# Low parts made by TensorE and ScalarE, a larger priority offset, and conv_out in two lots of token tiles, in a two-layer trunk

## The chip, the cores and the metric

One Trainium2 chip; the kernel is one launch on one of its cores. The metric is the device time of one execution in microseconds, the median of several runs. The engines are TensorE (PE; PEld is its weight load), VectorE (DVE), ScalarE (ACT), GpSimd (POOL) and SyncE (SP), which issues most of the DMAs. Each takes its own instructions in order and waits on semaphores for the others.

## The reference

1024 tokens of width 1024 pass two layers. Layer 0 mixes tokens with an S5 state-space model and a GLU, layer 1 with a gated short convolution. A SwiGLU FFN (hidden width 2816) and a per-layer input gate (PLE) follow each mixer, every sub-layer is normalised ahead, and all is float32.

```python
def shortconv_mixer(u, w_in, w_conv, w_out):
    b_gate, c_gate, v = jnp.split(u @ w_in, 3, axis=-1)
    cv = c_gate * v
    conv = lax.conv_general_dilated(cv, w_conv[:, None, :], ...)
    return (b_gate * conv) @ w_out

def swiglu_ffn(u, w_in, w_out):
    gate, up = jnp.split(u @ w_in, 2, axis=-1)
    return (jax.nn.silu(gate) * up) @ w_out
# per layer: x += mixer(rmsnorm(x)); x += ffn(rmsnorm(x)); x += ple(rmsnorm(x), p); last a final rmsnorm
```

## The kernel before, in words

**Precision.** Each float32 operand is split into a high part, a cast to fp32r on ScalarE, and a low part, the operand less its high part on VectorE (`split`, L86 to L88). A product is three matmuls: high by high, high by low, low by high (`mm3`, L121 to L124).

**Tiles.** The residual stream `h` is eight tiles of 128 tokens, t = 0 to 7, taken in the order 0, 4, 1, 5, 2, 6, 3, 7; tiles q and q + 4 are pair q. The phases are S5 and GLU, FFN 0 (in, out), PLE 0, conv_in, conv_out, FFN 1, PLE 1. `conv_in` and `ffn_in` use a block product of the Strassen kind (`block_product`, L289 to L318): seven products of half-size blocks in place of eight, with seven moving operands of 512 tokens, `moving(0)` to `moving(6)`. 0, 3 and 5 are plain blocks of the normalised tokens (p11, p21, p22); 1, 2, 4 and 6 are sums of blocks (T2, T1, T3, T4).

**The transitions.** `norm_pair` (L207 to L233) makes the moving operands of one pair. It normalises both tiles into `xn` (L173, VectorE; the statistic is L144 and L146 on VectorE and a power on GpSimd, L148), transposes them on TensorE into four PSUM tiles (L181), and from these makes b12 (a copy on ScalarE, L219), T1 (L221), T2 (L223), T3 (L228), T4 (L232) and the seven splits (`put`, by L87 and L88). p11 and p21 come from the pair's first tile, p12 and p22 from its second. PSUM has three buffers for p11, p12 and p22 (pool `tr`) and five for products and p21 (pool `mm`).

It runs at three places, where one phase hands its tokens to a block product: GLU to FFN 0, PLE 0 to conv_in, conv_out to FFN 1. Pairs 0, 1 and 2 follow tiles 1, 2 and 3, pair 3 follows tile 7, the last. Each moving operand spans all four pairs.

**Weights.** `weights_set` (L258 to L284) loads two raw tiles and makes the seven stationary operands `ws` from them: casts on ScalarE, subtractions at L88, and sums at L275, L276, L278 and L283 on VectorE. The raw tiles, the hidden tiles `ch` and the normalised tiles `xn` share a ring of four slots (`raw_tile`, L92).

**Order of the work.** The tile framework orders each engine's instructions by a simulated timeline and by priority. `first()` (L128) raises the priority of what it encloses by an offset: the statistics, `xn`, and each phase's last add into `h` (L503 in the GLU, L435 in PLE, L360 in conv_out). The order is fixed when the kernel is built.

**conv_out** (L541) goes through `out_phase` (L326): two groups of four weight units, and for each group all eight token tiles. Units 0 to 3 lie in `ulow`, one in each pair's part; units 4 to 7 are made between the first group's tiles. A tile's second group adds to `h`, takes the squares and calls `post`.

**split_pe** (L251 to L255), so far used in S5 alone, makes a low part without VectorE: the cast of the PSUM tile (L253), a matmul that adds minus the high part to the same PSUM tile (`identn` is minus the identity, L254), and a cast of what is left (L255).

Of the kernel before, what the change touches and what calls it, by code (L numbers as in the profile page):

```python
# [23 lines left out]
def trunk(  # L24
# [54 lines left out]
    hdram = dram.tile([T, P, D], F32, name="hd")  # L79
    hid = [dram.tile([T, P, 4, 2, P], F32, name=f"hid{i}") for i in range((NHT + 3) // 4)]  # L80

    def psum(pool=None):
        pool = pool or mm
        return pool.tile([P, 512], F32, name="ps" + pool.name, tag="ps")

    def split(hi, lo, src):  # L86
        A.copy(hi, src)  # L87
        V.tensor_tensor(lo, src, hi.bitcast(F32), ALU.subtract)  # L88
# [27 lines left out]
    def unit_of(slot, raw):  # L116
        hi, lo = slot
        split(hi, lo, raw)
        return hi, lo

    def mm3(ps, ahi, alo, bhi, blo, start, stop, more=False):  # L121
        PE.matmul(ps, ahi, bhi, start=start, stop=False, skip_group_check=more)  # L122
        PE.matmul(ps, ahi, blo, start=False, stop=False, skip_group_check=more)  # L123
        PE.matmul(ps, alo, bhi, start=False, stop=stop, skip_group_check=more)  # L124
# [2 lines left out]
    squares = {}  # L127

    def first():
        return tc.high_priority(offset=100)  # L130

    def square(t, cs):

        if "ms" not in squares:
            squares["ms"] = tiny.tile([P, T, 4], F32, name="ms", tag="ms")
        got = squares.setdefault(t, [])
        junk = t2_tile("junk", BF16, D)
        ms = squares["ms"][:, t, len(got):len(got) + 1]
# [25 lines left out]
    def act(kt, t):  # L164
        return act_view(kt, 0, t), act_view(kt, 1, t)
# [10 lines left out]
    def transposed(xn, hf, pool=None):  # L176

        pt = psum(pool or tr)
        for c in range(KH):
            kt = hf * KH + c  # L180
            PE.transpose(pt[:, c * P:(c + 1) * P], xn[:, kt * P:(kt + 1) * P], ident)  # L181
# [25 lines left out]
    def norm_pair(q, gb):  # L207
        t0, t1 = q, q + HT
        halves = 2 if q == HT - 1 else 1
        x0, x1 = normed(t0, gb, halves), normed(t1, gb, halves)  # L210

        def put(c, src):
            split(moving_part(c, 0, q), moving_part(c, 1, q), by_kt(src))

        p11, p12, p22 = transposed(x0, 0), transposed(x1, 0), transposed(x1, 1)
        p21 = transposed(x0, 1, mm)
        put(0, p11)
        b12 = t2_tile("b12")
        A.copy(b12, p12)  # L219
        T1 = t2_tile("T1")  # L220
        V.tensor_tensor(T1, b12, p11, ALU.subtract)  # L221
        T2 = t2_tile("T2")
        V.tensor_tensor(T2, p22, T1, ALU.subtract)  # L223
# [22 lines left out]
    def transposes(pt, parts):  # L246
        for c, a in enumerate(parts):
            PE.matmul(pt[:, c * P:(c + 1) * P], a, ident, start=c == 0, stop=True, is_transpose=True,
                      skip_group_check=c > 0)

    def split_pe(hi, lo, pt, view=lambda a: a):  # L251

        A.copy(hi, view(pt))  # L253
        PE.matmul(pt, identn, hi, start=False, stop=True, skip_group_check=True)  # L254
        A.copy(lo, view(pt))  # L255
# [114 lines left out]
    def room_low(q, s):  # L370
        return lambda: slot_low(q, s)
# [4 lines left out]
    def room_new(i):  # L376
        return lambda: slot_new(i)
# [37 lines left out]

    def ple(l, units, post):
        more, makers = ple_units(l, 1, [room_new(i) for i in range(4)])
        for nb in range(2):
            cs = slice(nb * 512, (nb + 1) * 512)
            if nb == 1:  # L420
                units = more
            for t in ORDER:
                upt = t2_tile("upt")
                nc.sync.dma_start(out=upt, in_=updram[l][:, t, cs])
                last = l == 1 and t == ORDER[-1] and nb == 1
                for c0, c1 in ((0, 256), (256, 512)) if last else ((0, 512),):
                    ps = psum()[:, 0:c1 - c0]
                    for kt in range(KT):
                        bhi, blo = units[kt // 2]
                        mm3(ps, *act(kt, t), bhi[:, kt % 2, c0:c1], blo[:, kt % 2, c0:c1], kt == 0, kt == KT - 1)  # L430
                    with first():
                        A.activation(ps, ps, AF.Sigmoid)
                        V.tensor_tensor(upt[:, c0:c1], ps, upt[:, c0:c1], ALU.mult)
                        hc = slice(nb * 512 + c0, nb * 512 + c1)
                        V.tensor_tensor(h[t][:, hc], upt[:, c0:c1], h[t][:, hc], ALU.add)  # L435
                        square(t, hc)
                if nb == 0 and makers:
                    makers.pop(0)()
                if nb == 1:
                    post(t)  # L440
# [40 lines left out]
    def glu(post):  # L481
        wg = s5_w_glu[0].rearrange("(kt p) (two n) -> p kt two n", p=P, two=2)
        rooms = [[room_high(i) for i in range(4)], [room_new(i) for i in range(4)],
                 [room_high(i) for i in (4, 5, 0, 1)], [room_new(i) for i in range(4)]]
        for nb in range(4):
            cs = slice(nb * 256, (nb + 1) * 256)
            units = []
            for u in range(KT // 2):
                raw = raw_tile()
                rv = raw.rearrange("p (kt two n) -> p kt two n", kt=2, two=2)  # L490
                for k in range(2):
                    nc.sync.dma_start(out=rv[:, k], in_=wg[:, 2 * u + k, :, cs])
                units.append([a.rearrange("p (kt n) -> p kt n", kt=2) for a in unit_of(rooms[nb][u](), raw)])
            for t in ORDER:
                ps = psum()
                for kt in range(KT):
                    bhi, blo = units[kt // 2]
                    mm3(ps, *act(kt, t), bhi[:, kt % 2, :], blo[:, kt % 2, :], kt == 0, kt == KT - 1)
                sg = t2_tile("sgg")[:, 0:256]
                with first():  # L500
                    A.activation(sg, ps[:, 256:512], AF.Sigmoid)
                    V.tensor_tensor(sg, ps[:, 0:256], sg, ALU.mult)
                    V.tensor_tensor(h[t][:, cs], sg, h[t][:, cs], ALU.add)  # L503
                    square(t, cs)
                if nb == 3:
                    post(t)
# [591 lines left out]
```

## Time and profile before

| | us |
|---|---|
| median of 3 runs | 2354.29 (2352.39 to 2357.11) |
| the profiled execution | 2359.43 |
| its span on the core | 2357.5 |
| TensorE busy | 2247.0 (95%) |
| VectorE busy | 1331.9 (56%) |
| ScalarE busy | 765.5 (32%) |
| GpSimd busy | 163.1 (7%) |

A row of the timeline gives start, duration, engine, line, operation, out<-in, form and count, and in brackets the idle time before it with what ended it. A row of the windows gives the window, its length, then for PE, PEld, DVE, ACT and POOL the busy time and in brackets the instructions, the granted TensorE clock, the DMA share and GB/s. A row of the waits gives who waited and for whom, the time in all, how often, and the longest. A row for one line of code gives the smallest, median and largest duration in ns. Matmuls overlap: one takes 0.39 us from its start, but the next starts 0.23 later.

### The profile page before, as it was taken

The page shows a single profiled execution, that of the slowest core. Times are in us where ns is not written, and L with a number is a line of the kernel's source. Part 1 is how long each engine was busy: PE and PEld are TensorE (multiplying, and loading weights), DVE is VectorE, ACT ScalarE, POOL GpSimd, SP SyncE. Part 2 cuts the span into 40 slices and gives each one's busy share as a digit, 9 for nine tenths or more (in the row PEclk, how much of TensorE's full clock was granted, in tenths as well). Part 3 has the DMA queues.
Part 4 walks back from the last instruction along what each step waited for, and adds up shares of the span by engine and source line. Part 5 has one row for each costly group of instructions (what it writes and reads, how often), then busy time and mean ns, then how long its engine had stood idle before and what let it go on. Part 6 is the DMA issues. An engine that isn't in the chain of part 4 may idle for free.

```text
span 2357.5 us, 27090 instructions
## 1 busy us (share of the span) xinstructions
PE 2247.0 (95%) x10253; PEld 1835.7 (78%) x10253; DVE 1331.9 (56%) x2246; ACT 765.5 (32%) x1449; POOL 163.1 (7%) x268
## 2 busy tenths in 40 slices
PE   6888999899999999999979999989999999999998
PEld 4776887788888878878858888768888888788787
DVE  7785326866666642125488776487666666121454
ACT  6554223433333320013343332153333333000232
POOL 2110001000000000000000000010000001000000
PEclk8999999999999999999989999999999999999999
DMA  7555202333333364333232225434333335543333
GB/s 246 141 135 148 69 1 89 105 112 112 111 114 110 107 241 149 118 127 114 70 129 81 90 92 179 159 125 125 108 108 107 111 113 172 212 139 107 108 109 110
DMA packets 212978, 288.87 MB, mean 123 GB/s; under 512 B 21360, under 2 KB 152432, under 8 KB 212848
## 3 DMA queue, kind: packets, MB, share of 16 engines
q1 hardware_dynamic: 191520, 212.63, 29.0%
q0 software_dynamic: 20928, 74.47, 10.2%
q8 instruction: 80, 1.31, 0.2%
q14 instruction: 50, 0.41, 0.1%
q10 hardware_dynamic: 400, 0.04, 0.0%
HBM read 190.93 MB, written 79.69 MB: 115 GB/s over the span
## 4 chain that ended last, share of the span: by engine, by line
PE 85%; DMA 6%; DVE 5%; ACT 1%; SPq 1%; issue 1%; POOL 0%; DVEq 0%; POOLq 0%; ACTq 0%
PE psmm L122 27%; PE psmm L124 27%; PE psmm L123 27%; DMA ch<-hid 2%; PE pstr L181 1%; DMA raw<-in_ffn_w_out_dram 1%; DMA tw<-tmp 1%; DVE W L575 1%; DVE gv L925 1%; DMA h<-hd 1%; DVE tmp L575 1%; DVE ulow L88 1%; DVE uhigh L88 1%; PE pstr L874 0%; DVE raw L575 0%
## 5 line engine op out<-in xcount | busy, mean ns | idle before, releaser
L122 PE MATMUL psmm<-ulow,ws 128*128 128x512 f32 x896 | 351.1, 393 | 1.6 <-ACT s L301 1.6
L123 PE MATMUL psmm<-ulow,ws 128*128 128x512 f32 x896 | 350.6, 391 | 0.0
L124 PE MATMUL psmm<-ulow,ws 128*128 128x512 f32 x896 | 350.4, 391 | 0.0
L124 PE MATMUL psmm<-uhigh,ws 128*128 128x512 f32 x672 | 265.3, 395 | 0.0
L122 PE MATMUL psmm<-uhigh,ws 128*128 128x512 f32 x672 | 265.1, 394 | 0.0
L123 PE MATMUL psmm<-uhigh,ws 128*128 128x512 f32 x672 | 264.9, 394 | 0.0
L360 DVE TENSOR_TENSOR h<-psmm,h 128x512 f32<-128x512 f32 x128 | 88.0, 690 | 276.6 <-PE psmm L124 276.6
L88 DVE TENSOR_TENSOR ws<-raw,ws 128x512 fp32r<-128x512 f32 x224 | 153.6, 688 | 117.8 <-ACT ws L87 117.4
L87 ACT CAST ws<-raw 128x512 fp32r<-128x512 f32 x224 | 137.5, 619 | 213.0 <-PE psmm L124 211.2
L122 PEld LDWEIGHTS psmm<-ulow,ws 128*128 128x128 f32 x896 | 169.4, 189 | 39.5 <-ACT s L301 2.9
L123 PEld LDWEIGHTS psmm<-ulow,ws 128*128 128x128 f32 x896 | 169.4, 189 | 36.2
L124 PEld LDWEIGHTS psmm<-ulow,ws 128*128 128x128 f32 x896 | 169.2, 189 | 36.2
L87 ACT CAST ws<-st 128x512 fp32r<-128x512 f32 x168 | 104.0, 620 | 204.4 <-PE psmm L124 189.5
L123 PEld LDWEIGHTS psmm<-uhigh,ws 128*128 128x128 f32 x672 | 126.1, 188 | 30.3
L124 PEld LDWEIGHTS psmm<-uhigh,ws 128*128 128x128 f32 x672 | 126.1, 188 | 30.3
L122 PEld LDWEIGHTS psmm<-uhigh,ws 128*128 128x128 f32 x672 | 126.1, 188 | 29.1
L323 POOL DMA_DIRECT2D hid<-hs x104 | 78.2, 755 | 903.4 <-DVE hs L88 895.4
L122 PE MATMUL psmm<-ulow,ch 128*128 128x512 f32 x320 | 128.4, 401 | 10.8 <-DMA ch<-hid 10.8
L139 ACT ACTIVATE junk<-h 128x512 bf16<-128x512 f32 (+1 forms) x113 | 64.0, 567 | 204.0 <-DVE h L360 104.0
L87 ACT CAST uhigh<-raw 128x1024 fp32r<-128x1024 f32 x36 | 37.2, 1049 | 278.9 <-PE psmm L124 136.7
L123 PE MATMUL psmm<-ulow,ch 128*128 128x512 f32 x320 | 127.6, 399 | 0.0
L124 PE MATMUL psmm<-ulow,ch 128*128 128x512 f32 x320 | 127.5, 398 | 0.0
(240 smaller groups left out, 4238.5 us busy)
## 6 DMA issues: line engine op xcount, KB each, us to landing
hid<-hs POOLq DMA_DIRECT2D x104, 512.0 KB, 4.3
ch<-hid SPq DMA_DIRECT2D x96, 512.0 KB, 3.7
raw<-in_ffn_w_in_dram SPq DMA_DIRECT2D x88, 512.0 KB, 4.4
raw<-in_ffn_w_out_dram SPq DMA_DIRECT2D x44, 512.0 KB, 3.6
hd<-h POOLq DMA_DIRECT2D x24, 512.0 KB, 3.0
h<-hd SPq DMA_DIRECT2D x24, 512.0 KB, 8.7
raw<-in_conv_w_in_dram SPq DMA_DIRECT2D x24, 512.0 KB, 4.0
up<-ev SPq DMA_DIRECT2D x32, 256.0 KB, 3.2
```

The costliest lines, as they stand in the source:

```text
L87: A.copy(hi, src)
L88: V.tensor_tensor(lo, src, hi.bitcast(F32), ALU.subtract)
L122: PE.matmul(ps, ahi, bhi, start=start, stop=False, skip_group_check=more)
L123: PE.matmul(ps, ahi, blo, start=False, stop=False, skip_group_check=more)
L124: PE.matmul(ps, alo, bhi, start=False, stop=stop, skip_group_check=more)
L139: A.activation(junk[:, cs], h[t][:, cs], AF.Square, scale=1.0 / math.sqrt(D), accum_out=ms)
L181: PE.transpose(pt[:, c * P:(c + 1) * P], xn[:, kt * P:(kt + 1) * P], ident)
L323: nc.gpsimd.dma_start(out=hid[ht // 4][half * HT:(half + 1) * HT, :, ht % 4].rearrange("t p l j -> p t l j"), in_=hs.bitcast(F32))
L360: V.tensor_tensor(h[t][:, cs], ps[nb], h[t][:, cs], ALU.add)
L575: V.tensor_tensor(o, a, b, op)
L925: V.tensor_tensor_scan(gv[:, g, 1:P], dec, sv[:, g, 1:P], 0.0, ALU.mult, ALU.add)
```

## The change

Four edits. (1) `put` may make a low part by `split_pe`, and does so for the plain blocks, operands 0, 3 and 5; the transposes are written as matmuls (`transposes`); T1 stands ahead of operand 0 in the code, T4 ahead of operand 3. (2) The offset of `first()` goes from 100 to 400. (3) The loops of the GLU and PLE are flattened. (4) conv_out has its own loop: token tiles 0, 4, 1, 5 take both groups of weights, then 2, 6, 3, 7; units 0 to 3 lie in the parts of pairs 2 and 3 of `ulow` alone, and units 4 to 7 are made during the first lot's first group. In the new file the lines of before shift: T1 is L230, T2 L233, T4 L237, T3 L240, the transposes L258, split_pe L263 to L265, `mm3` L123 to L125, the sums of `weights_set` L285, L286, L288 and L293, the low parts L89, `xn` L174, the last adds L516 (GLU), L442 (PLE) and L576 (conv_out).

```diff
 def first():
-    return tc.high_priority(offset=100)
+    return tc.high_priority(offset=400)
...
-        def put(c, src):
-            split(moving_part(c, 0, q), moving_part(c, 1, q), by_kt(src))
-
-        p11, p12, p22 = transposed(x0, 0), transposed(x1, 0), transposed(x1, 1)
-        p21 = transposed(x0, 1, mm)
-        put(0, p11)
+        def put(c, src, on_pe=False):
+            hi, lo = moving_part(c, 0, q), moving_part(c, 1, q)
+            if on_pe:
+                split_pe(hi, lo, src, by_kt)
+            else:
+                split(hi, lo, by_kt(src))
+
+        def part(xn, hf, pool=tr):
+            pt = psum(pool)
+            transposes(pt, [xn[:, (hf * KH + c) * P:(hf * KH + c + 1) * P] for c in range(KH)])
+            return pt
+
+        p11, p12, p22 = part(x0, 0), part(x1, 0), part(x1, 1)
+        p21 = part(x0, 1, mm)
         b12 = t2_tile("b12")
         A.copy(b12, p12)
         T1 = t2_tile("T1")
         V.tensor_tensor(T1, b12, p11, ALU.subtract)
+        put(0, p11, True)
         T2 = t2_tile("T2")
         V.tensor_tensor(T2, p22, T1, ALU.subtract)
         put(1, T2)
         put(2, T1)
-        put(3, p21)
+        T4 = t2_tile("T4")
+        V.tensor_tensor(T4, p21, T2, ALU.subtract)
+        put(3, p21, True)
         T3 = t2_tile("T3")
         V.tensor_tensor(T3, p22, b12, ALU.subtract)
         put(4, T3)
-        put(5, p22)
-        T4 = t2_tile("T4")
-        V.tensor_tensor(T4, p21, T2, ALU.subtract)
+        put(5, p22, True)
         put(6, T4)
...
     def conv_out(post):
-        rooms = [(room_low(q, 0), False) for q in range(HT)] + [(room_new(i), True) for i in range(4)]
-        hts = [(ct, *room) for ct, room in enumerate(rooms)]
-        out_phase(conv_w_out[0].rearrange("(ht p) n -> ht p n", p=P), [hts[0:4], hts[4:8]], post)
+        rooms = [room_low(2 + i // 2, i % 2) for i in range(4)] + [room_new(i) for i in range(4)]
+        units = {}
+        def make(ct):
+            units[ct] = unit_of(rooms[ct](), load_raw(conv_w_out[0, ct * P:(ct + 1) * P], "p n -> p n"))
+        for ct in range(KH):
+            make(ct)
+        for i, t in [(i, t) for ts in (ORDER[:4], ORDER[4:]) for i in range(2) for t in ts]:
+            ch = raw_tile(shape=(P, 4, 2, P), dt=F32R, name="ch")
+            nc.sync.dma_start(out=ch.bitcast(F32), in_=hid[i][t])
+            if i == 0:
+                nc.sync.dma_start(out=h[t], in_=hdram[t])
+            for nb in range(2):
+                ...
+            if len(units) < KT:
+                make(len(units))
+            if i == 1:
+                post(t)
```

The order in which the engines get their instructions changes with it. On TensorE, at the end of the GLU, before: the last matmuls of the GLU (`w`, the GLU's weights), the transposes of pairs 2 and 3, and the first product of FFN 0 (`ulow,ws`).

```order
L123 MATMUL psmm<-w_3164,ulow 128x512
L124 MATMUL psmm<-w_3164,ulow 128x512
L181 MATMUL pstr<-ident,xn 128x128 x8
L181 MATMUL psmm<-ident,xn 128x128 x4
L181 MATMUL pstr<-ident,xn 128x128 x12
L122 MATMUL psmm<-ulow,ws 128x512
L123 MATMUL psmm<-ulow,ws 128x512
L124 MATMUL psmm<-ulow,ws 128x512
```

Afterwards the same place, with the identity matmuls (`identn`):

```order
L124 MATMUL psmm<-w_3164,ulow 128x512
L125 MATMUL psmm<-w_3164,ulow 128x512
L258 MATMUL psmm<-ident,xn 128x128 x4
L258 MATMUL pstr<-ident,xn 128x128 x4
L264 MATMUL pstr<-ulow,identn 128x512
L264 MATMUL psmm<-ulow,identn 128x512
L264 MATMUL pstr<-uhigh,identn 128x512
L258 MATMUL pstr<-ident,xn 128x128 x8
L264 MATMUL pstr<-ulow,identn 128x512
L123 MATMUL psmm<-ulow,ws 128x512
L124 MATMUL psmm<-ulow,ws 128x512
L125 MATMUL psmm<-ulow,ws 128x512
```

Part of the transposes stands ahead of the GLU's last matmuls now (above these rows), three identity matmuls of pair 2 stand behind them, and after the last eight transposes comes one of pair 3, p11's, ahead of the first product.

On VectorE at the same place, before: from T1's low part of pair 2 to the last tile's `xn` (L173). L501 to L503 are the GLU's gate and last add; `T_` and a number is T1, T3 or T4.

```order
L88 TENSOR_TENSOR ulow<-T_3548,ulow 128x4x128
L275 TENSOR_TENSOR st<-raw 128x512
L88 TENSOR_TENSOR ulow<-T_3550,ulow 128x4x128
L502 TENSOR_TENSOR sgg<-psmm,sgg 128x256
L88 TENSOR_TENSOR uhigh<-T_3558,uhigh 128x4x128
L88 TENSOR_TENSOR uhigh<-pstr,uhigh 128x4x128
L88 TENSOR_TENSOR uhigh<-T_3564,uhigh 128x4x128
L276 TENSOR_TENSOR raw<-raw 128x512
L503 TENSOR_TENSOR h<-sgg,h 128x256
L278 TENSOR_TENSOR st<-raw 128x512
L146 TENSOR_TENSOR ms<-ms 128x1
L173 SCALAR_TENSOR_TENSOR xn<-h,rs,gb 128x512 x2
```

Afterwards:

```order
L89 TENSOR_TENSOR ulow<-T_3552,ulow 128x4x128
L285 TENSOR_TENSOR st<-raw 128x512
L89 TENSOR_TENSOR ulow<-T_3557,ulow 128x4x128
L89 TENSOR_TENSOR uhigh<-T_3563,uhigh 128x4x128
L286 TENSOR_TENSOR raw<-raw 128x512
L515 TENSOR_TENSOR sgg<-psmm,sgg 128x256
L89 TENSOR_TENSOR uhigh<-T_3568,uhigh 128x4x128
L288 TENSOR_TENSOR st<-raw 128x512
L516 TENSOR_TENSOR h<-sgg,h 128x256
L147 TENSOR_TENSOR ms<-ms 128x1
L174 SCALAR_TENSOR_TENSOR xn<-h,rs,gb 128x512 x2
```

The subtraction `uhigh<-pstr` is gone here, as are two further up, and L288 (L278 of before) stands ahead of the last add instead of behind it.

On VectorE at the end of conv_out, before: from the last low parts of pair 2 in `ulow` to the weight operations behind the last `xn`.

```order
L88 TENSOR_TENSOR ulow<-T_11515,ulow 128x4x128
L144 TENSOR_SCALAR ms<-ms 128x1
L275 TENSOR_TENSOR st<-raw 128x512
L88 TENSOR_TENSOR uhigh<-T_11523,uhigh 128x4x128
L88 TENSOR_TENSOR uhigh<-pstr,uhigh 128x4x128
L88 TENSOR_TENSOR uhigh<-T_11529,uhigh 128x4x128
L146 TENSOR_TENSOR ms<-ms 128x1
L276 TENSOR_TENSOR raw<-raw 128x512
L173 SCALAR_TENSOR_TENSOR xn<-h,rs,gb 128x512 x2
L278 TENSOR_TENSOR st<-raw 128x512
L88 TENSOR_TENSOR ws<-raw,ws 128x512
```

Afterwards, from the last add of conv_out on (L576):

```order
L576 TENSOR_TENSOR h<-psmm,h 128x512
L145 TENSOR_SCALAR ms<-ms 128x1
L89 TENSOR_TENSOR uhigh<-T_11552,uhigh 128x4x128
L89 TENSOR_TENSOR uhigh<-T_11557,uhigh 128x4x128
L285 TENSOR_TENSOR st<-raw 128x512
L147 TENSOR_TENSOR ms<-ms 128x1
L286 TENSOR_TENSOR raw<-raw 128x512
L174 SCALAR_TENSOR_TENSOR xn<-h,rs,gb 128x512 x2
L288 TENSOR_TENSOR st<-raw 128x512
L230 TENSOR_TENSOR T_11638<-b_11636,pstr 128x512
L89 TENSOR_TENSOR ws<-raw,ws 128x512
```

The three low parts that stood behind the sum of two weight blocks (L275) are gone or ahead of it (now L285), and the statistic (L147) follows the sum at once; two adds of conv_out that stood ahead of pair 2's operations now stand among them.

More of the change, by code (lines that the diff above doesn't have):

```diff
@@ L417, in ple @@
         more, makers = ple_units(l, 1, [room_new(i) for i in range(4)])
-        for nb in range(2):
+        for nb, t in [(nb, t) for nb in range(2) for t in ORDER]:
             cs = slice(nb * 512, (nb + 1) * 512)
-            if nb == 1:
[L421 to L440, printed above, removed]
+            upt = t2_tile("upt")
+            nc.sync.dma_start(out=upt, in_=updram[l][:, t, cs])
+            last = l == 1 and t == ORDER[-1] and nb == 1
+            for c0, c1 in ((0, 256), (256, 512)) if last else ((0, 512),):
+                ps = psum()[:, 0:c1 - c0]
+                for kt in range(KT):
+                    bhi, blo = (units, more)[nb][kt // 2]
+                    mm3(ps, *act(kt, t), bhi[:, kt % 2, c0:c1], blo[:, kt % 2, c0:c1], kt == 0, kt == KT - 1)
+                with first():
+                    A.activation(ps, ps, AF.Sigmoid)
+                    V.tensor_tensor(upt[:, c0:c1], ps, upt[:, c0:c1], ALU.mult)
+                    hc = slice(nb * 512 + c0, nb * 512 + c1)
+                    V.tensor_tensor(h[t][:, hc], upt[:, c0:c1], h[t][:, hc], ALU.add)
+                    square(t, hc)
+            if makers:
+                makers.pop(0)()
+            if nb == 1:
+                post(t)
     def up_load(l, pools, tags):
@@ L484, in glu, with make @@
                  [room_high(i) for i in (4, 5, 0, 1)], [room_new(i) for i in range(4)]]
-        for nb in range(4):
+        units = {}
+        def make(nb):
             cs = slice(nb * 256, (nb + 1) * 256)
-            units = []
+            units[nb] = []
             for u in range(KT // 2):
@@ L492, in glu @@
                     nc.sync.dma_start(out=rv[:, k], in_=wg[:, 2 * u + k, :, cs])
[L493 to L506, printed above, removed]
+                units[nb].append([a.rearrange("p (kt n) -> p kt n", kt=2) for a in unit_of(rooms[nb][u](), raw)])
+        for nb, t in [(nb, t) for nb in range(4) for t in ORDER]:
+            if nb not in units:
+                make(nb)
+            cs = slice(nb * 256, (nb + 1) * 256)
+            ps = psum()
+            for kt in range(KT):
+                bhi, blo = units[nb][kt // 2]
+                mm3(ps, *act(kt, t), bhi[:, kt % 2, :], blo[:, kt % 2, :], kt == 0, kt == KT - 1)
+            sg = t2_tile("sgg")[:, 0:256]
+            with first():
+                A.activation(sg, ps[:, 256:512], AF.Sigmoid)
+                V.tensor_tensor(sg, ps[:, 0:256], sg, ALU.mult)
+                V.tensor_tensor(h[t][:, cs], sg, h[t][:, cs], ALU.add)
+                square(t, cs)
+            if nb == 3:
+                post(t)
     def conv_in(cvq):
@@ L541, in conv_out @@
     def conv_out(post):
-        rooms = [(room_low(q, 0), False) for q in range(HT)] + [(room_new(i), True) for i in range(4)]
-        hts = [(ct, *room) for ct, room in enumerate(rooms)]
-        out_phase(conv_w_out[0].rearrange("(ht p) n -> ht p n", p=P), [hts[0:4], hts[4:8]], post)
+        rooms = [room_low(2 + i // 2, i % 2) for i in range(4)] + [room_new(i) for i in range(4)]
+        units = {}
+        def make(ct):
[8 more added lines that the diff above has]
+            for nb in range(2):
+                cs = slice(nb * 512, (nb + 1) * 512)
+                ps = psum()
+                for k in range(KH):
+                    bhi, blo = units[i * KH + k]
+                    mm3(ps, ch[:, k, 0], ch[:, k, 1], bhi[:, cs], blo[:, cs], k == 0, k == KH - 1)
+                with first():
+                    V.tensor_tensor(h[t][:, cs], ps, h[t][:, cs], ALU.add)
+                    if i == 1:
+                        square(t, cs)
+            if len(units) < KT:
+                make(len(units))
+            if i == 1:
+                post(t)
     R0, R1 = slice(0, NP), slice(NP, P)
```

## The prediction

> **What bounds the kernel now.** I read the page's first lines, then who TensorE waits for, then busy time by stage.
>
> ```profile
> span 2357.5 us, 27090 instructions
> PE 2247.0 (95%) x10253; PEld 1835.7 (78%) x10253; DVE 1331.9 (56%) x2246; ACT 765.5 (32%) x1449; POOL 163.1 (7%) x268
> PE pstr L181 <- DVE xn L173: 36.0, 5, 10.7
> PE psmm L122 <- ACT s L301: 1.6, 3, 0.7
> 375.00:430.00 55.00, 43.90 (x213) 36.22 (x212) 45.48 (x80) 26.82 (x58) 6.78 (x12) 0.91 0.35 115
> 1236.00:1460.00 224.00, 224.00 (x977) 183.00 (x976) 164.69 (x245) 73.18 (x114) 14.05 (x29) 1.00 0.31 96
> 1520.00:1580.00 60.00, 49.06 (x235) 40.26 (x234) 50.00 (x88) 30.82 (x67) 8.53 (x14) 0.91 0.44 149
> ```
>
> TensorE is busy for 95% of the span; in the long products (1236 to 1460) it has no gap. Its largest single wait is for the normalised last tile, `xn`: 36.0 us in five waits. The change touches the three places where these lie: the end of the GLU (375 to 430), the end of PLE 0 (near 1225) and the end of conv_out (1520 to 1580). The windows of the first and last hold 11.1 and 10.9 us of idle TensorE. So TensorE's timeline at the three places comes next.
>
> ```profile
> 406.32 0.39 PE L124 MATMUL psmm<-w,ulow 128*128 128x512 f32 x1
> 407.88 0.66 PE L181 MATMUL pstr<-ident,xn 128*128 128x128 f32 x4
> 418.95 1.97 PE L181 MATMUL pstr<-ident,xn 128*128 128x128 f32 x8 [10.42 <-DVE xn L173]
> 421.15 0.63 PE L123 MATMUL psmm<-ulow,ws 128*128 128x512 f32 x1
> 423.28 0.60 PE L122 MATMUL psmm<-ulow,ws 128*128 128x512 f32 x1
> 423.71 0.40 PE L123 MATMUL psmm<-ulow,ws 128*128 128x512 f32 x1
> 423.95 0.39 PE L124 MATMUL psmm<-ulow,ws 128*128 128x512 f32 x1
> 1207.80 1.09 PE L181 MATMUL pstr<-ident,xn 128*128 128x128 f32 x8 [1.45 <-DVE xn L173]
> 1211.89 0.80 PE L181 MATMUL pstr<-ident,xn 128*128 128x128 f32 x4 [3.00 <-DVE xn L173]
> 1223.97 1.97 PE L181 MATMUL pstr<-ident,xn 128*128 128x128 f32 x8 [10.39 <-DVE xn L173]
> 1226.16 0.63 PE L123 MATMUL psmm<-ulow,ws 128*128 128x512 f32 x1
> 1556.74 0.40 PE L124 MATMUL psmm<-w,ch 128*128 128x512 f32 x1
> 1569.69 1.97 PE L181 MATMUL pstr<-ident,xn 128*128 128x128 f32 x8 [10.71 <-DVE xn L173]
> 1571.88 0.63 PE L123 MATMUL psmm<-ulow,ws 128*128 128x512 f32 x1
> ```
>
> The row that ends each idle time transposes the last tile; the L122 to L124 rows behind it are the first product. I measure each place by the start of that product's second matmul (L123), which is the first to read a low part. VectorE and ScalarE show why it can start at once.
>
> ```profile
> 407.86 0.69 DVE L221 TENSOR_TENSOR T<-b,pstr 128x512 f32<-128x512 f32 x1 [0.78 <-ACT b L219]
> 418.15 1.41 DVE L173 SCALAR_TENSOR_TENSOR xn<-h,rs,gb 128x512 f32<-128x512 f32 x2 [0.75 <-POOL rs L148]
> 423.09 0.68 DVE L221 TENSOR_TENSOR T<-b,pstr 128x512 f32<-128x512 f32 x1
> 408.57 0.59 ACT L87 CAST ulow<-pstr 128x512 fp32r<-128x512 f32 x1
> ```
>
> The high part of the last pair's plain block p11 is cast at 408.57, ten microseconds before the last tile; p11 comes from the pair's first tile and waits for nothing else. T1 of the last pair (423.09) needs the last tile, and the first product doesn't read it.
>
> **The change part by part.** The sums are made on the profiled execution, 2359.43 us (span 2357.5); the median of the three runs, 2354.29, is 5.14 lower, and I subtract that at the end.
>
> (a) The lower wait. In the new code p11's low part is made inside p11's own PSUM tile, so it can only be made after T1 has read p11, and its identity matmul stands on TensorE ahead of the first product. At each place the path from the last `xn` becomes: transposes, b12, T1, hi cast, identity matmul, lo cast, second matmul. The operations that no row shows there have rows elsewhere:
>
> ```profile
> L254 PE MATMUL pstr<-ulow,identn x24: 394/497/792, 8.6 to 224.1; 128*128 128x512 f32 x24
> L255 ACT CAST ulow<-pstr x24: 567/587/627, 9.5 to 227.4; 128x512 fp32r<-128x512 f32 x24
> 1223.17 1.41 DVE L173 SCALAR_TENSOR_TENSOR xn<-h,rs,gb 128x512 f32<-128x512 f32 x2 [0.75 <-POOL cvp L527]
> 1228.44 0.68 DVE L221 TENSOR_TENSOR T<-b,pstr 128x512 f32<-128x512 f32 x1
> 1568.88 1.42 DVE L173 SCALAR_TENSOR_TENSOR xn<-h,rs,gb 128x512 f32<-128x512 f32 x2 [0.46 <-POOL rs L148]
> 1571.51 0.69 DVE L221 TENSOR_TENSOR T<-b,pstr 128x512 f32<-128x512 f32 x1
> 1571.38 0.62 ACT L87 CAST ws<-st 128x512 fp32r<-128x512 f32 x1
> 1571.90 1.14 ACT L87 CAST ws<-raw 128x512 fp32r<-128x512 f32 x2
> ```
>
> T1 starts 4.94 us after `xn` at the GLU and 5.27 at PLE, since six weight operations stand ahead of it on VectorE, in the new order too; 2.63 at conv_out. Behind it come 0.69 + 0.59 + 0.50 + 0.59 = 2.4. So the second matmul follows `xn` by 7.3 and 7.7 us, against 3.00 and 2.99 now: +4.3 and +4.7. At conv_out T1 isn't what ends last: ScalarE has five weight casts between b12 and the hi cast, and four others between hi and lo. Its casts start 0.52 apart (1571.38 to 1571.90), the first 2.5 us after `xn`; ten steps bring lo to 2.5 + 5.2 = 7.7, and it ends at 8.3, against 3.00: +5.3. Bounds: without ScalarE's queue conv_out has 2.63 + 2.4 = 5.0 (+2.0); with the matmul at 0.79 each place is 0.3 more.
>
> (b) The last tile earlier. 36 subtractions leave VectorE, three per pair. Its operations start 0.60 apart (the next fence: 14 steps in 8.39). At the GLU 13 operations stand between T1 of the third pair and the last tile's add (L503), afterwards 11: -1.2. T1 itself stands after the last transposes, which move ahead of the last three matmuls (-0.7) but behind six identity matmuls of the first two pairs (+1.4). Net -0.5. At PLE the rows are
>
> ```profile
> 1212.33 0.68 DVE L223 TENSOR_TENSOR T<-pstr,T 128x512 f32<-128x512 f32 x1
> 1220.72 0.68 DVE L435 TENSOR_TENSOR h<-upt,h 128x512 f32<-128x512 f32 x1
> 1565.26 0.69 DVE L275 TENSOR_TENSOR st<-raw 128x512 f32<-128x512 f32 x1 [1.83 <-DMA raw<-in_ffn_w_in_dram]
> ```
>
> From T2 to the add stand 14 steps, 11 afterwards: -1.8. T2 itself comes 1.1 to 1.5 earlier, because three low parts fewer stand ahead of the tile before (the 1.45 wait at 1207.80 goes): -3.1 together, the first pairs' identity matmuls being swallowed by that wait. At conv_out VectorE waits until 1565.26 for a weight tile and has three low parts behind it (3 x 0.60) before the statistic of the last tile; afterwards the statistic follows at once, -1.8, and the weight tile, whose slot comes free earlier, lands perhaps a microsecond earlier: -2.9. Bounds: -1.8, the load landing no earlier; -6.3, the load never waited for (the last matmul ends at 1557.1, six identity matmuls later 1558.5; the add, two low parts and L285 follow by 1560.7, and `xn` 1.9 behind that start, which is 1568.88 - 1565.26 less 1.8 for the three low parts: 1562.6 against 1568.88).
>
> (c) Identity matmuls: 36, twelve a place. Six are counted in (b), the third pair's and p11's stand where TensorE is idle, and two of the last pair stand in the product at a pitch of 0.24 (423.71 to 423.95): +0.5 a place, 1.0 if each took its 0.50. If the idle time ahead were gone, the other four would cost 1.0 a place.
>
> (d) The clock. After 1.45 us of idle eight transposes took 1.09, after 3.00 four took 0.80, after 10.4 eight took 1.97; matmuls then start 0.43 apart (423.28 to 423.71) until 4.76 us after the first transpose, against 0.24. Now the transposes and six matmuls at the GLU lie in that stretch. Afterwards some 3 to 4 us of idle lie between transposes and product, and the product begins the stretch anew: up to eleven slow matmuls, 11 x 0.19 = 2.1 instead of 1.1. I take +0.5 a place, bounds 0 and +0.9. [...]
>
> (e) The waits for `s` (L301), 1.6 in three: they arise because product 3 follows product 0 into one tile; in the new order other products lie between. -0.7, -0.7, -0.2.
>
> (f) conv_out's start. Units 4 to 7 are now wanted after four tiles, not eight.
>
> ```profile
> 1440.00:1471.60 31.60, 11.67 (x48) 9.01 (x48) 1.00 0.73 249
> 1479.82 0.47 PE L122 MATMUL psmm<-ulow,ch 128*128 128x512 f32 x1 [2.20 <-DMA ch<-hid]
> 1482.23 1.23 DVE L88 TENSOR_TENSOR w<-raw,w 128x1024 fp32r<-128x1024 f32 x1 [3.81 <-ACT w L87]
> 1486.30 1.22 DVE L88 TENSOR_TENSOR w<-raw,w 128x1024 fp32r<-128x1024 f32 x1
> ```
>
> TensorE already waits there, 2.2 us for a hidden tile. Of the matmuls that read hidden tiles, 24 a token tile, 48 lie before 1471.6 (the windows row, of those alone), so the tile that starts at 1479.82 is the fourth. It ends 24 x 0.23 = 5.5 later, at 1485.4. The last two units are ready at 1483.4 and 1487.5, which the old order has time for; in the new one unit 7 is first read nine matmuls into the fifth tile, at 1487.5, just as it is ready. On VectorE the subtractions of units 4 and 5 stand behind one more add than before, and the loads of units 6 and 7 wait for them. I take +0.5, bounds -2 (the tile wait goes) and +6 (each of the two is late by 3 us, about one load and cast).
>
> (g) The priority offset and the flattened PLE and GLU loops: what they do to the order is in (a) to (f); elsewhere the order on each engine is all but that of before, so nothing, and no queue but those named is passed.
>
> Sum: GLU -0.5 + 4.3 + 0.5 + 0.5 - 0.7 = +4.1; PLE -3.1 + 4.7 + 0.5 + 0.5 - 0.7 = +1.9; conv_out's end -2.9 + 5.3 + 0.5 + 0.5 - 0.2 = +3.2; its start +0.5. Together +9.7: 2359.43 becomes 2369.1, and the median 2354.29 becomes 2364.0, 0.4% slower. A measurement of this kernel tells about 0.2%, 4.7 us, from no change: the band is 2349.6 to 2359.0.
>
> **The rivals.**
> R1, faster: VectorE's backlog goes altogether. The last add would then follow the last matmul, and `xn` would start 3.5 us after it (the add 0.7, GpSimd's power 0.75 as the bracket before `xn` has it, and an estimated 2.0 for gate, square and statistic). With (a) behind it the second matmul comes 3.5 + 7.3 = 10.8 after them, against 421.15 - 406.7 = 14.4 now: -3.6 at the GLU and PLE, -2.6 at conv_out, +3.0 for (c), in all -6.8: 2347.5. It decides when fewer than about five operations stand between the last T1 and the last add. For it: conv_out's order is near this. Against: the GLU and PLE keep eleven.
> R2, not slower: conv_out reaches its bound of -6.3 because the load lands before it is wanted, 3.4 better, and the clock costs nothing (-1.5). 9.7 - 4.9 = +4.8, 2359.1, at the edge of the band; with ScalarE's casts out of the way too, since their weight tile came earlier (+2.0, not +5.3), 2355.8. It turns on when that load lands; for it, its ring slot is freed earlier; against, the row at 1565.26 still waits for that very load.
> R3, slower still: conv_out's units 6 and 7 come late, +6 in place of +0.5: 2369.5. For it, the two rows at 1482 and 1486; against, loads of one tile land in a few microseconds.
> R4: the low parts aren't waited for, as if the product ran other matmuls first. (a) falls to T1's own cost, zero: 9.7 - 14.3 = -4.6, 2349.7. Against it stands TensorE's order, in which the identity matmul is ahead of every product.
>
> **How the numbers follow.** Forecast 0.45, R1 0.08, R2 0.22, R3 0.15, R4 0.10. Faster by over 0.2%: R1 and half of R4 and a little for what I don't see, 0.17. Within: R2, half of R4 and the lower edge of the forecast, 0.28. Slower: the rest, 0.55. Range 2350 to 2370: from R4 to just over R3; the forecast's own is 2359 to 2369 by the bounds of (b), (d) and (f).
>
> **What would show it.** Right: at the three places the waits for `xn` shrink to about 8 to 10 us, and new waits of 3 to 4 us appear on TensorE for the hi cast (L263) ahead of the identity matmul, with 0.6 for the lo cast (L265) behind it. The chain of waits then runs through T1 (L230). Wrong: T1 starts within 2.5 us of `xn` at the GLU and PLE; the second matmul of the product starts less than 5 us after `xn`; or conv_out's wait for `xn` falls under 5 us.

## The result, and the profile after

The changed kernel takes 2365.89 us (median of 6 runs, 2363.09 to 2367.50) against 2355.12 for the kernel before on the same chip (6 runs): ratio 1.0046, 95% interval 1.0033 to 1.0058. It is 10.8 us slower; the forecast was 9.7 us slower. In the experiments below, one of the six runs of e4 took 4545.57 us, almost twice the others, and is left out of its median.

The page of the changed kernel and its table of whom TensorE waits for:

```profile
span 2365.1 us, 27193 instructions
PE 2259.4 (96%) x10289; PEld 1845.7 (78%) x10289; DVE 1315.2 (56%) x2210; ACT 782.9 (33%) x1485; POOL 163.0 (7%) x268
PE psmm L123 <- DMA ch<-hid: 19.8, 5, 5.1
PE pstr L258 <- DVE xn L174: 17.7, 4, 5.3
PE pstr L264 <- ACT ulow L263: 11.0, 6, 3.8
```

VectorE has 36 instructions fewer (2210 for 2246) and 16.7 us less to do, and the wait for `xn` has halved, from 36.0 to 17.7 us. The time that went there came back in three forms: a new wait of 11.0 us for the high cast ahead of the identity matmul (L264), a TensorE that is busy for longer (2259.4 us for 2247.0: the 36 identity matmuls, and more work at a granted clock of 0.50: at the GLU 7.60 us between 417.39 and 428.69, before 4.75 between 418.95 and 423.71), and one long wait for a hidden tile (5.1). The waits for hidden tiles as a whole did not grow in this profile (19.8 us, 19.9 before): the start of FFN 0's output happens to wait 2.7 us where it waited 4.6.

The end of the GLU on TensorE, then VectorE and ScalarE at the same place:

```profile
417.39 1.94 PE L258 MATMUL pstr<-ident,xn 128*128 128x128 f32 x8 [5.14 <-DVE xn L174]
422.79 0.80 PE L264 MATMUL pstr<-ulow,identn 128*128 128x512 f32 x1 [3.46 <-ACT ulow L263]
423.38 0.63 PE L123 MATMUL psmm<-ulow,ws 128*128 128x512 f32 x1
424.26 0.79 PE L124 MATMUL psmm<-ulow,ws 128*128 128x512 f32 x1 [0.25 <-ACT ulow L265]
428.96 0.85 PE L123 MATMUL psmm<-ulow,ws 128*128 128x512 f32 x3
```

```profile
416.49 1.41 DVE L174 SCALAR_TENSOR_TENSOR xn<-h,rs,gb 128x512 f32<-128x512 f32 x2 [0.75 <-POOL rs L149]
421.44 0.68 DVE L230 TENSOR_TENSOR T<-b,pstr 128x512 f32<-128x512 f32 x1
422.15 0.58 ACT L263 CAST ulow<-pstr 128x512 fp32r<-128x512 f32 x1
423.62 0.58 ACT L265 CAST ulow<-pstr 128x512 fp32r<-128x512 f32 x1 [0.37 <-PE pstr L264]
```

Read them as one chain: `xn` at 416.49, T1 4.95 us later at 421.44, the high cast as soon as T1 has ended (422.15), the identity matmul (422.79), the low cast (423.62), the second matmul (424.26). From `xn` to the second matmul it is 7.77 us, where it was 3.00. (The transposes wait 5.14 us for `xn` and no longer 10.42, but not because the last tile comes sooner: identity matmuls and the waits for their casts now lie in that idle time.) PLE 0 shows the same chain, 8.09 us (1220.05 to 1228.14) where it was 2.99:

```profile
1220.95 1.94 PE L258 MATMUL pstr<-ident,xn 128*128 128x128 f32 x8 [5.30 <-DVE xn L174]
1226.68 0.79 PE L264 MATMUL pstr<-ulow,identn 128*128 128x512 f32 x1 [3.79 <-ACT ulow L263]
1228.14 0.80 PE L124 MATMUL psmm<-ulow,ws 128*128 128x512 f32 x1 [0.25 <-ACT ulow L265]
1220.05 1.41 DVE L174 SCALAR_TENSOR_TENSOR xn<-h,rs,gb 128x512 f32<-128x512 f32 x2 [0.75 <-POOL cvp L540]
1225.32 0.68 DVE L230 TENSOR_TENSOR T<-b,pstr 128x512 f32<-128x512 f32 x1
```

At the end of conv_out T1 comes early (1573.88, 2.64 after `xn`) and it is ScalarE's queue that sets the casts; `xn` to the second matmul is 8.27 us (two further high by high matmuls run ahead of it meanwhile). On TensorE, VectorE and ScalarE:

```profile
1563.97 0.39 PE L125 MATMUL psmm<-w,ch 128*128 128x512 f32 x1
1572.14 1.94 PE L258 MATMUL pstr<-ident,xn 128*128 128x128 f32 x8 [5.23 <-DVE xn L174]
1576.98 0.80 PE L264 MATMUL pstr<-ulow,identn 128*128 128x512 f32 x1 [2.90 <-ACT ulow L263]
1579.51 0.79 PE L124 MATMUL psmm<-ulow,ws 128*128 128x512 f32 x1
1571.24 1.42 DVE L174 SCALAR_TENSOR_TENSOR xn<-h,rs,gb 128x512 f32<-128x512 f32 x2 [0.46 <-POOL rs L149]
1573.88 0.69 DVE L230 TENSOR_TENSOR T<-b,pstr 128x512 f32<-128x512 f32 x1 [0.62 <-ACT b L228]
1576.35 0.58 ACT L263 CAST ulow<-pstr 128x512 fp32r<-128x512 f32 x1
1578.86 0.59 ACT L265 CAST ulow<-pstr 128x512 fp32r<-128x512 f32 x1
```

conv_out's start has the one wait that the forecast had not seen. TensorE, SyncE and the chain of waits of the changed kernel, and then SyncE and the chain of before:

```profile
1483.45 0.74 PE L123 MATMUL psmm<-ulow,ch 128*128 128x512 f32 x1 [5.10 <-DMA ch<-hid]
1467.54 2.49 SPq L568 DMA_DIRECT2D h<-hd  x5
1472.78 7.39 SPq L566 DMA_DIRECT2D ch<-hid  x2
1472.78 10.54 DMA ch<-hid
```

```profile
1466.05 1.86 SPq L348 DMA_DIRECT2D h<-hd  x3
1471.29 0.32 SPq L346 DMA_DIRECT2D ch<-hid  x1
1471.29 8.40 DMA ch<-hid
```

The fourth hidden tile takes 10.54 us from issue to landing. Five loads of `h` were issued just ahead of it on SyncE's queue; before there were three, and it took 8.40. Behind the wait of 5.10 the matmuls start slowly (0.74), where after 2.20 they did not (0.47).

**By place.** The profiles are cut at events that every kernel has: the GLU's multiplication on VectorE for the last tile ahead of its last column block, one store of a hidden tile in FFN 0, the eighth multiplication of PLE 0, the last GpSimd operation of conv_in, one store in FFN 1. Between them, in us:

| | start to GLU's last block | GLU to FFN 0 | FFN 0 | PLE 0 and conv_in | conv_out to FFN 1 |
|---|---|---|---|---|---|
| before | 359.17 | 360.89 | 438.85 | 282.35 | 505.76 |
| after | 356.94 | 366.45 | 434.39 | 285.15 | 511.47 |

The three places that the change touches cost 5.6 + 2.8 + 5.7 = 14.1 us. The two stretches that it doesn't touch happen to be 6.7 us shorter in this profile; over the eleven profiles without the last experiment the first lies between 354.65 and 359.17 and FFN 0 between 434.39 and 438.85. So a place is read from these stretches only where several profiles agree, and the medians decide on the whole.

### The profile page after: what moved, and what is told of

It is laid out like the page before. It is cut to its first block, busy times and chain, and to the rows that moved or that the text cites. A ratio compares the mean times of both kernels' runs of the same rounds, so it can differ in the third digit from the quotient of the medians.

```text
span 2365.1 us, 27193 instructions
## 1 busy us (share of the span) xinstructions
PE 2259.4 (96%) x10289; PEld 1845.7 (78%) x10289; DVE 1315.2 (56%) x2210; ACT 782.9 (33%) x1485; POOL 163.0 (7%) x268
## 4 chain that ended last, share of the span: by engine, by line
PE 85%; DMA 6%; DVE 6%; ACT 1%; issue 1%; SPq 0%; POOL 0%; DVEq 0%; POOLq 0%; ACTq 0%
PE psmm L123 27%; PE psmm L124 27%; PE psmm L125 27%; DMA ch<-hid 2%; DMA tw<-tmp 1%; DMA raw<-in_ffn_w_out_dram 1%; DVE W L613 1%; DVE gv L963 1%; PE pstr L182 1%; PE pstr L258 0%; DVE tmp L613 0%; PE pstr L978 0%; DMA raw<-in_ffn_w_in_dram 0%; PE pstr L912 0%; PE pstr L264 0%
## 5 line engine op out<-in xcount | busy, mean ns | idle before, releaser
L123 PE MATMUL psmm<-ulow,ws 128*128 128x512 f32 x896 | 351.3, 393 | 0.0
L125 PE MATMUL psmm<-ulow,ws 128*128 128x512 f32 x896 | 350.6, 392 | 0.0
L125 PE MATMUL psmm<-uhigh,ws 128*128 128x512 f32 x672 | 265.6, 395 | 0.0
L123 PE MATMUL psmm<-uhigh,ws 128*128 128x512 f32 x672 | 265.2, 395 | 0.0
L89 DVE TENSOR_TENSOR ws<-raw,ws 128x512 fp32r<-128x512 f32 x224 | 154.0, 689 | 121.3 <-ACT ws L88 121.2
L370 DVE TENSOR_TENSOR h<-psmm,h 128x512 f32<-128x512 f32 x96 | 66.1, 690 | 243.0 <-PE psmm L125 242.9
L123 PEld LDWEIGHTS psmm<-ulow,ws 128*128 128x128 f32 x896 | 169.9, 190 | 36.9 <-ACT ulow L88 0.5
L125 PEld LDWEIGHTS psmm<-ulow,ws 128*128 128x128 f32 x896 | 169.6, 189 | 35.9
L125 PEld LDWEIGHTS psmm<-uhigh,ws 128*128 128x128 f32 x672 | 126.1, 188 | 30.2
L123 PEld LDWEIGHTS psmm<-uhigh,ws 128*128 128x128 f32 x672 | 126.2, 188 | 29.0
L123 PE MATMUL psmm<-ulow,ch 128*128 128x512 f32 x320 | 127.9, 400 | 11.4 <-DMA ch<-hid 11.4
L124 PE MATMUL psmm<-uhigh,ch 128*128 128x512 f32 x320 | 126.7, 396 | 0.9 <-DVE uhigh L89 0.9
L124 PE MATMUL psmm<-ulow,ch 128*128 128x512 f32 x320 | 127.6, 399 | 0.0
```

Source lines behind the costliest of these rows:

```text
L370: V.tensor_tensor(h[t][:, cs], ps[nb], h[t][:, cs], ALU.add)
```

## The experiments

Theory A: the first product now waits for the low part of p11, which is made behind T1. Rivals: the new conv_out carries the cost (B); VectorE, the identity matmuls or the clock carry it (C). All ratios below are against the kernel before on the same chip, five rounds each. e1 to e11 ran on one chip, e12 and e13 on another, where the kernel before took 2354.61 us and not 2355.51 to 2356.32, so across the two only ratios are compared. The offset of 400 alone leaves every engine's order in the kernel before word for word as it was, and so do the flattened loops of the GLU and PLE: they cost and gain nothing by themselves, and where two kernels differ in them and in conv_out, conv_out is the difference.

### e1: the split alone

```diff
 # the kernel before, and:
-    norm_pair of before
+    norm_pair of the change (put(0), put(3), put(5) by split_pe)
```

> The kernel before with the split alone (plain blocks' low parts by TensorE and ScalarE, T1 ahead of operand 0); conv_out and the offset as before. Theory A (the first product waits for p11's low part behind T1): the cost appears without the rest of the change, GLU +4 to +5.5, PLE +2 to +3, conv_out's end +2 to +3, in all +8 to +11 us, 2363 to 2366. Rival B (the new conv_out costs most of what the change costs): at most +5, 2360 or less.

2366.03 us, ratio 1.0042 (1.0028 to 1.0056): the whole cost of the change, without its conv_out. By place it is 4.7 (365.58), 4.1 (286.49) and 3.1 (508.86) us, 11.9 together. A holds, B falls for the main part.

### e3: the new conv_out alone

```diff
-        rooms = [(room_low(q, 0), False) for q in range(HT)] + [(room_new(i), True) for i in range(4)]
-        ...
-        out_phase(..., [hts[0:4], hts[4:8]], post)
+        for i, t in [(i, t) for ts in (ORDER[:4], ORDER[4:]) for i in range(2) for t in ts]:
+            ...
```

> The kernel before with the new conv_out alone; all low parts by VectorE as before. Theory A: conv_out's start loses about 4 us (one hidden tile queued behind the loads of h), its end gains 3 to 5 by the shorter queue on VectorE ahead of the last tile, so within 2 us of before, 2353 to 2357. Rival B: +5 or more, 2360 or over.

2359.52 us, ratio 1.0018 (1.0009 to 1.0026), +4.0: more than expected, since the end of conv_out did not win back what its start lost. The stretch of conv_out grows by 3.5 us (509.21), and the start has the same wait as in the changed kernel:

```profile
1476.67 0.76 PE L122 MATMUL psmm<-ulow,ch 128*128 128x512 f32 x1 [5.78 <-DMA ch<-hid]
```

e1 and e3 add up to +14.5, the change has +10.8: the two parts aren't independent at conv_out's end, or the runs' scatter hides it.

### e4: p11 by VectorE again

```diff
         p21 = part(x0, 1, mm)
+        put(0, p11)
         b12 = t2_tile("b12")
         ...
-        put(0, p11, True)
```

> The changed kernel with one thing undone: p11's low part (operand 0) again by VectorE and ahead of T1 in the code; p21 and p22 still by TensorE and ScalarE. Theory A: the first product no longer waits for T1, -4 us at the GLU and PLE and -3 at conv_out, +0.6 a place for the subtraction that comes back: -9 us against the changed kernel, 2357, and in the trace no identity matmul between the last transposes and the first product. Rival C (the identity matmuls and the clock, not the wait, are the cost): 24 of 36 identity matmuls stay, so at most -4, 2362.

2361.78 us, ratio 1.0029 (1.0017 to 1.0042): 4.1 us better than the changed kernel, not 9. C's number, but not its reason. The identity matmul is gone from in front of the first product, and that product starts right behind the transposes; then TensorE stops again one product later. TensorE, VectorE and ScalarE at the GLU's end:

```profile
416.80 0.78 PE L123 MATMUL psmm<-ulow,ws 128*128 128x512 f32 x1
424.93 1.65 PE L123 MATMUL psmm<-ulow,ws 128*128 128x512 f32 x3 [3.15 <-ACT ulow L88]
423.55 0.68 DVE L233 TENSOR_TENSOR T<-pstr,T 128x512 f32<-128x512 f32 x1
424.26 0.62 ACT L88 CAST ulow<-T 128x512 fp32r<-128x512 f32 x1 [1.85 <-DVE T L233]
```

The wait is for the high part of T2, which needs the last tile. Before, the product of p21 came between; p21 is the other block of the pair's first tile and was split as early as p11. Theory A was too narrow. A2: p11 and p21 need nothing of the last tile, and their two products, 24 matmuls, covered the making of T1 and T2. The split by TensorE makes both wait for T1, T2 and T4.

### e8 and e9: p22 alone by TensorE and ScalarE

```diff
         p21 = part(x0, 1, mm)
+        put(0, p11)
         ...
-        put(0, p11, True)
         ...
+        put(3, p21)
         T4 = t2_tile("T4")
         V.tensor_tensor(T4, p21, T2, ALU.subtract)
-        put(3, p21, True)
```

e8 is the changed kernel with this edit, e9 the kernel before with the same norm_pair and its own conv_out.

> The changed kernel with p11 and p21 by VectorE again, ahead of T1 and T4 as before; p22 alone by TensorE and ScalarE. Theory A2 (p11 and p21 come from the pair's first tile, and their two products, 24 matmuls, covered the making of T1 and T2; undoing p11 alone left the second product waiting for T2's high part): no wait over 0.7 us between the last transposes and the products, GLU and PLE back to before, conv_out's start still +3 to +4: 2358 to 2360. Rival C (identity matmuls and the clock): 12 identity matmuls stay, about 2361.

> The kernel before with p22 alone by TensorE and ScalarE, conv_out and offset as before. Theory A2: one subtraction a pair leaves VectorE, 0.6 us off the way to the last tile at each place, nothing waits for p22's low part: -2 to 0 us, 2353 to 2356. Rival: identity matmuls cost more than the tile gains, +1 to +3, 2357 to 2359.

e8: 2356.24 us, ratio 0.9998 (0.9989 to 1.0007), 9.7 us better than the changed kernel, and better than the 2358 to 2360 expected. e9: 2352.18 us, ratio 0.9983 (0.9974 to 0.9991), faster than before. The places of e9 are 361.35, 280.30 and 505.82, 1.5 us less than before in all, so its 4 us aren't fully placed. In the engines' order only the new conv_out stands between e8 and e9: 4.1 us. p11 and p21, then, carry the cost of the split: without theirs it is gone, though p22's twelve identity matmuls stay.

### e11: the split for the first three pairs only

```diff
         p21 = part(x0, 1, mm)
+        if q == HT - 1:
+            put(0, p11)
+            put(3, p21)
         ...
-        put(0, p11, True)
+        if q < HT - 1:
+            put(0, p11, True)
         ...
-        put(3, p21, True)
+        if q < HT - 1:
+            put(3, p21, True)
         ...
-        put(5, p22, True)
+        put(5, p22, q < HT - 1)
```

> The kernel before with the split of the change for the first three pairs, and all low parts of the last pair by VectorE ahead of T1; conv_out as before. Theory A2 (only the last pair's detour costs): no wait for a low part ahead of the first product, 27 of the 36 identity matmuls stay but nine a place cost at most 0.23 each and some lie in idle time: 2354 to 2358, against 2366 when the last pair has the split too. Rival C (identity matmuls, ScalarE's casts and the clock carry the cost): 2361 to 2364.

2356.22 us, ratio 0.9997 (0.9989 to 1.0005). It differs from e1 in the last pair alone and is 9.8 us faster: the cost lies in the last pair, and 27 of the 36 identity matmuls, with the work that they take off VectorE, make no difference that can be measured. The row that has the identity matmul and its wait in the changed kernel is not there; on TensorE the product follows the transposes:

```profile
418.96 1.94 PE L262 MATMUL pstr<-ident,xn 128*128 128x128 f32 x8 [4.87 <-DVE xn L173]
420.55 0.78 PE L122 MATMUL psmm<-ulow,ws 128*128 128x512 f32 x1
421.12 0.63 PE L123 MATMUL psmm<-ulow,ws 128*128 128x512 f32 x1
421.98 0.49 PE L122 MATMUL psmm<-ulow,ws 128*128 128x512 f32 x1
422.31 0.39 PE L123 MATMUL psmm<-ulow,ws 128*128 128x512 f32 x1
```

It also says that the split gains nothing here: of the idle 10.4 us before the last transposes half is now filled with identity matmuls and waits for them, but the last tile comes no earlier.

### e7 and e10: the second lot's loads of h held back

```diff
             if i == 0:
+                if t not in ORDER[:4]:
+                    G.tensor_copy(h[t][:, 0:1], h[ORDER[0]][:, 0:1])
                 nc.sync.dma_start(out=h[t], in_=hdram[t])
```

The load overwrites the copied column, so the result is as before, but it must wait until the first tile has been added. e7 has it in the changed kernel, e10 in e3.

> The changed kernel with the loads of h for conv_out's second lot held back until the first lot's first tile is added (a one-column copy on GpSimd that the load overwrites). Theory A for conv_out's start (the fourth hidden tile took 10.5 us from issue to landing because five loads of h stood ahead of it in the queue): the wait of 5.1 us falls to under 1.5 and the slow clock behind it goes, -3 to -5 us, 2361 to 2363. Rival D (weight units 6 and 7 are late, or the hidden tile's slot): the wait stays at 4 to 5 us or a wait for a weight unit takes its place, and the time stays at 2366.

> The kernel before with the new conv_out and the loads of h for its second lot held back; low parts by VectorE. Against the new conv_out alone (2359.5): if the hidden tile queued behind five loads of h is what that costs, -3 to -5 us, 2355 to 2357, and the wait of 5.8 us at its fourth tile falls under 2. Rival: the wait only moves to a later tile, 2359.

e10: 2355.89 us, ratio 0.9998 (0.9989 to 1.0007), 3.6 us better than e3, with intervals that don't meet. TensorE and SyncE:

```profile
1470.84 0.47 PE L122 MATMUL psmm<-ulow,ch 128*128 128x512 f32 x1 [1.27 <-DMA ch<-hid]
1484.91 1.74 SPq L557 DMA_DIRECT2D h<-hd  x4
```

The wait falls from 5.78 to 1.27 and the matmul behind it takes 0.47 and no longer 0.76; four of the eight loads of `h` now go out at 1484.91. So it was the loads ahead in the queue, not the weight units: with the low parts made as before, the new conv_out costs 4 us by these loads, and when they are held back it is worth the same as the old one. It agrees with this that the fourth tile took 10.54 us with five loads ahead of it (the changed kernel) and 8.40 with three (before). By what means such loads hold a tile up is not shown.

e7: 2365.46 us, ratio 1.0045 (1.0032 to 1.0058), no better than the changed kernel as far as the runs can tell, against -3 to -5 expected. The wait for the fourth hidden tile did fall, from 5.10 to 1.76, with a new one of 1.73 later:

```profile
1481.76 0.47 PE L123 MATMUL psmm<-ulow,ch 128*128 128x512 f32 x1 [1.76 <-DMA ch<-hid]
1507.78 0.51 PE L123 MATMUL psmm<-w,ch 128*128 128x512 f32 x1 [1.73 <-DMA ch<-hid]
```

Its stretch of conv_out is 3.3 us shorter (508.17); its FFN 0 is 3.0 us longer than in the changed kernel's profile (437.36), where the same code ran. Whether that is chance stays open. It fits with this that the changed kernel (2365.89) isn't slower than e1 (2366.03), which has the old conv_out. So in the medians the 4 us of the new conv_out show where the low parts of p11 and p21 are VectorE's (e3, e8, e10) and not beside the whole split; the intervals, some 3 us either way, leave room for them.

### e12 and e13: what is left over, and the same loads elsewhere

```diff
 # e12: e8 with the late loads of e7.  e13: e9, and in out_phase:
                 if gi == 0:
+                    if t not in ORDER[:3]:
+                        G.tensor_copy(h[t][:, 0:1], h[ORDER[ORDER.index(t) - 3]][:, 0:1])
                     nc.sync.dma_start(out=h[t], in_=hdram[t])
```

> p22 alone by TensorE and ScalarE, the new conv_out, and its second lot's loads of h held back: what the runs so far left of the change. If the parts add up (p22 alone with the old conv_out 2352.2; the new conv_out with h held back gave 0 against the old one), 2351 to 2353, and conv_out's two lots are worth nothing by themselves. Rival: with the last tile earlier the two lots gain what they could not before, 2348 to 2350.

> p22 alone by TensorE and ScalarE, the old conv_out, and the loads of h held back by three tiles wherever a phase starts on stored hidden tiles (both FFN outputs and conv_out). If the loads of h ahead of the hidden tiles cost there too, the waits for hidden tiles at FFN 0's output (4.6 us, with the slow clock behind it) and at conv_out's start (2.2) shrink: -3 to -5 us against 2352.2, 2347 to 2349. Rival: the transfer itself is the limit there (weights, h and hidden tiles together), so the wait stays and the time is 2351 to 2353.

e12: 2351.66 us, ratio 0.9984 (0.9974 to 0.9993), level with e9, as the sum of its parts has it. e13: 2337.67 us, ratio 0.9928 (0.9914 to 0.9941). By the ratios (0.9928 against 0.9983) that is some 13 us under e9, about three times what was expected; the medians, from two chips, differ by 14.5. By place the profile of e13 is 6.1 us shorter in FFN 0, 3.6 from conv_out to FFN 1 and 7.0 behind that, where FFN 1's output lies, and TensorE's waits for hidden tiles fall, e9 first, then e13:

```profile
PE psmm L122 <- DMA ch<-hid: 20.7, 7, 4.8
PE psmm L122 <- DMA ch<-hid: 9.1, 3, 4.1
```

The windows at the start of both FFN outputs, e9 first, then e13 (window, length, busy PE, PEld, DVE, ACT, POOL, clock, DMA share, GB/s):

```profile
836.00:900.00 64.00, 60.16 (x252) 48.25 (x252) 23.24 (x28) 10.46 (x12) 2.81 (x4) 0.97 0.73 263
1960.00:2040.00 80.00, 74.92 (x317) 60.19 (x316) 32.62 (x40) 18.91 (x25) 5.08 (x7) 0.98 0.63 223
```

```profile
836.00:900.00 64.00, 64.00 (x276) 51.48 (x275) 23.05 (x27) 11.60 (x13) 4.65 (x9) 1.00 0.70 259
1960.00:2040.00 80.00, 80.00 (x346) 64.69 (x345) 31.78 (x38) 17.65 (x21) 5.42 (x10) 1.00 0.64 231
```

In these windows TensorE has no gap in e13 and its clock stays at 1.00: 24 and 29 matmuls more in the same time, at about the same GB/s. The rival, that the transfer itself is the limit, falls: the same bytes in another order leave no wait there.

## Why the prediction was right, and where it was not

**The low part's wait (a)** held in mechanism and size: 7.77, 8.09 and 8.27 us from `xn` to the second matmul, against 7.3, 7.7 and 8.3. Shown by e1 and e11: with the last pair's split +10.5 us, without it nothing; and by e8, where p11 and p21 go back to VectorE. Of the signs that were named, the waits for the high cast came (3.46, 3.79, 2.90) and T1 started where it was to start. The waits for `xn` fell further than said, to 5.1 to 5.3 and not 8 to 10: at the GLU because the third pair's identity matmuls and the waits for their casts stand in that time, at conv_out because the tile comes earlier. The wait for the low cast was 0.25 at the GLU and PLE 0, not 0.6. What it missed is p21: I had the first product alone in view, and e4 shows that the second would have waited as well.

**The last tile (b)** was mis-sized. At the GLU `xn` comes 59.55 us after the table's mark where it came after 58.98, so 0.6 late where I had 0.5 early: two operations fewer stand ahead of it, but one of those left, L285, now waits 0.79 us for its weight tile:

```profile
410.58 0.69 DVE L285 TENSOR_TENSOR st<-raw 128x512 f32<-128x512 f32 x1 [0.79 <-DMA raw<-in_ffn_w_in_dram]
```

At PLE 0 it comes 2.0 early (62.27 for 64.26), not 3.1. At conv_out it starts 7.27 after the last matmul began instead of 12.14, 4.9 early, where -2.9 and the +1.4 of identity matmuls made -4.3.

**The identity matmuls (c)** aren't measured alone: e11, with 27 of them and 27 subtractions fewer on VectorE, is level with before, so they cost no more than those gain.

**The clock (d)**, taken at +0.5 a place between the bounds of 0 and +0.9, was right in sum and wrong by place. At the GLU the slow stretch runs from 422.79 to 428.69, 5.9 us where it was 4.76 before, both at a granted clock of 0.50, and from the product's second matmul on there are ten slow steps (one of 0.59, nine of 0.43) where there were six; at about 0.2 each, and more for the first, that is 1.0, not 0.5, and just over the bound of 0.9. At PLE 0 there are six (1228.14 to 1230.87) where there were seven (1226.16 to 1229.15), so nothing; at conv_out's end it is 0.5 (1579.51 to 1582.23 and one step of 0.35, before 1571.88 to 1574.02). Together that is the 1.5 of the sum.

**The waits for `s` (e)** are gone from the changed kernel's table of waits, as said.

**conv_out's start (f)** is the step whose reason failed: "I take +0.5". It costs 3.5 (e3 by place) to 4.1 (e8 against e9), inside the bound of 6 but for another reason. The prediction looked at weight units 6 and 7; the wait was for a hidden tile behind loads of `h` that the new loop lets SyncE issue all at once, as e10 shows. In the changed kernel itself the profile has this cost, the medians of e1 and e7 don't; that stays open.

**The rivals.** R1 and R2 needed the last tile much earlier; it came 4.9 us earlier at conv_out, 2.0 at PLE 0 and not at all at the GLU. R3 came close to its price (4 of 6 us, in e3 and e8) by the loads of `h`. R4 was excluded by TensorE's order, as said. In the changed kernel's profile the places cost 14.1 for a forecast of 9.7, most of the difference by (f); that the median came out at +10.8, so near the forecast, is in part luck: single terms were off by up to 3 us, and stretches that the change doesn't touch came out shorter. The split's own part is no luck: the forecast without (f) is +9.2, and e1, though with the old conv_out, has 11.9 by place and +10.5 by its median.

## What to carry to other kernels

Before work moves off a busy engine, ask what the last operands of the stage need: a way round that costs the busy engine less can still make an operand that was ready early wait for the one that comes last, and then only the last round matters (here one pair in four carried all of the cost, and the other three neither cost nor gained). Early operands are cover for late ones, so count how many of them the change leaves. And look at what stands ahead of a needed transfer in its queue before looking at its size: holding back loads that weren't needed yet was worth some 13 us, more than everything else here.

## What the runs showed of the hardware

A hidden tile of 512 KB took 8.40 us with three loads of the same size issued ahead of it on the same queue and 10.54 with five, where the median for such a tile is 3.7 on the page of before and 3.8 on that of the changed kernel. In the kernel before, after pauses of TensorE of 10.42, 10.39 and 10.71 us, the slow clock lasted from the first transpose on 4.76 us at the GLU (418.95 to 423.71), 5.18 at PLE 0 (1223.97 to 1229.15) and 4.33 at conv_out's end (1569.69 to 1574.02), with a granted clock of 0.50 in all three. At the GLU of the changed one, where the transposes were followed by a second pause of 3.46 us, it lasted 5.9 from the identity matmul on (422.79 to 428.69), at 0.50 too. In e11 it lasted 3.0 us from the first transpose (418.96 to 421.98), after identity matmuls at 411.50 and 413.29. So its length is not one number here, even for the same instructions (4.33 to 5.18 in the kernel before), and an estimate for this kernel should carry 3 to 6 us.
